# Seven small products spread over a pair of columns, partial sums kept in PSUM and copied by ScalarE

## The chip, the cores and the metric

The kernel runs on one core of a Trainium2 chip. A core has five engines that run side by side and meet at semaphores: TensorE (PE in the profile; PEld is its weight load), VectorE (DVE), ScalarE (ACT), GpSimd (POOL) and SyncE (SP, here only a queue of transfers). Matmuls write to the banks of PSUM; everything else lies in SBUF or in the chip's large memory. The metric is the device time of one execution in microseconds (us). A change is told from no change here when it is over 0.5%.

## The reference

One layer of a hybrid decoder, for 1024 prompt rows and 64 sample rows (T = 1088 columns in the kernel, where rows are laid along the free axis):

```python
h = rmsnorm(x) * (1 + scale) + shift
[u_pool | z_pool | z_ssm | xBC | dt | g] = h @ w_in            # 1024 -> 8224 columns
P = (pool_mix(u_pool) * silu(z_pool)) @ w_pool_out
S = gated_rmsnorm(SSD(conv(xBC)) + D*x, z_ssm) @ w_ssm_out
x = x + gate * ((sigmoid(g_pool) * P + sigmoid(g_ssm) * S) @ w_o)
y = rmsnorm(x)
```

The change lies wholly in the stage that computes `h @ w_in`. All is fp32; a product is made of three products of rounded halves (high by high, high by low, low by high), for which weights and activations are each split in a high and a low part (`whi` and `wlo` for weights).

## The kernel before

**Pairs of columns.** `w_in` is cut into columns of 128. Two columns make a pair, and a pair is computed as a 2 by 2 block product: the two columns, the two halves of the inner dimension (4 tiles of 128 each), and the two halves of T (HF = 544, each again cut into two halves of SB = 272). By Strassen's scheme in Winograd's form seven products do instead of eight. They are named after their weight operand: `b11`, `b21`, `t2`, `t3`, `d12`, `t4`, `b22`. `product` (L430) makes one: for each half `s`, 12 matmuls of 128x128 weights on 272 columns into one bank, and then `use(s, p)` takes the bank's content out. The weight operands are sums of blocks, made by `diff` (L353, on DVE, one on POOL); `split` (L145 on ACT for the high part, L148 on POOL or DVE for the low part) brings them into one of four `whi` and four `wlo` buffers.

**Kinds of pair.** 31 pairs are computed: one inside the opening stage, then `light[1]` and the first of the woven list as plain pairs with seven products (kind None), then 28 that go two by two, a pair of kind "a" and its mate of kind "b". For these the `b21` product is left out of `strassen` (six products), and the `b21` products of both pairs together are made by a second Strassen level: `burst` (L490) computes seven sub-products of six matmuls each, L496, on operands `J` that `joint_operands` prepared. It leaves the part for "a" in `ra` (buffer `c2`) and that for "b" in `rb`. The burst runs as a block of its own ahead of the six products of "a"; its weights are made by `joint_steps` from two loads of their own (`raw`, 256 KB each, one of which holds data that the column's own load brings too).

**Where results go.** In `strassen` (L517) each product's bank is taken out as it ends: `b11` is copied to SBUF by ACT (L532) and, in pairs "a" and "b", added by DVE to `ra` or `rb` (L525); `t2` and `t3` are added by DVE to what stands in SBUF (L520); `d12` and `t4` give outputs (DVE, L525), and `b22` is accumulated on the bank of `d12` ("chained") and gives the last one. Where the destination wants a function (Silu, Sigmoid), ACT applies it in place afterwards (L527). The kernel holds eight PSUM banks in three pools: three `mm` (`PA`), four `ps` (`PB`) and one `pc` (`PC`). Products take them in turn, PA, PB, PA, PB, PA, PB, PC, and in the last ten pairs PB and PA alternately.

**Ticks.** A pair's generator yields after a product. At each yield `between` lets later work of earlier pairs go one step (convolution: L1220 on ACT, three L1223 on DVE, L1228 on ACT) and at `n` = 3, 4, 5 a step of the next pair's weights. A pair "a" yields 10 times, "b" 6 times. Beside the first 20 pairs each yield also moves `splits` (L282, L283 on ACT, L285 on POOL: 40 later weight tiles are split and stored) at a pace of 19/5 ticks a job. Beside the last ten pairs it moves first the preparation of `dt` (14 ticks) and then the sample rows of the state-space branch (`all_samples`, 28 steps); `samples_beside` spreads them by the count `8 * LAST`, with `LAST` = 10.

**Order.** The program is traced in the order of the code, and a scheduler that simulates the engines and goes by priorities lays out each engine's queue; evictions and weight splits have high priority. From tick 14 of the last ten pairs on, PE's order is that of the code (`in_line`). Each engine works off its queue in order.

Of the kernel before, what the change touches and what calls it, by code (L numbers as in the profile page):

```python
# [11 lines left out]
ALU = mybir.AluOpType  # L12
# [34 lines left out]
def tile_pool_ssd_step(  # L47
# [213 lines left out]
    def splits():  # L261
# [68 lines left out]
    def pair_w(c0, c1, pri, apart, meta):  # L330
        def run():
            joint = []
# [21 lines left out]

            def steps():
                add("b11", b11)
# [4 lines left out]
                t4 = raw_()  # L361
                add("t2", t2)
                if meta["kind"] is None:
                    add("b21", b21)
# [9 lines left out]
            def part(x, *names):  # L374
                with tc.high_priority(pri):
                    hi, lo = split(x, highs, n=2 * len(names), eng=V)
                for i, n in enumerate(names):
                    jw[n] = hi[:, 2 * i:2 * i + 2], lo[:, 2 * i:2 * i + 2]

            def joint_steps():  # L380
                wa, wb = joint
                tt = raw_()
                diff(tt[:, 2:4], wb[:, 2:4], wb[:, 0:2])
                diff(tt[:, 0:2], tt[:, 2:4], wa[:, 0:2], ALU.add)
                yield
                part(wa, "b11", "b21")
                diff(wb[:, 0:2], wb[:, 0:2], wa[:, 0:2])
                part(tt, "t2", "t3")
                diff(wa[:, 2:4], tt[:, 0:2], wa[:, 2:4])
                yield  # L390
                part(wb, "d12", "b22")
                part(wa[:, 2:4], "t4")
                yield
# [18 lines left out]
            if apart:  # L412
                add("b11", b11)
                prep_q.append(apart_())
            elif meta["kind"] == "a":
                prep_q.append(joint_steps())
# [2020 lines left out]
```

## Time and profile before

| what | value |
|---|---|
| median of 3 runs | 1271.7 us (1266.74 to 1272.05) |
| the profiled execution, device time | 1262.98 us |
| its span, first to last instruction | 1261.3 us |
| mean granted TensorE clock | 0.993 |
| opening stage (norm, modulation, first pair) | 0 to about 90 us |
| woven pairs (`light[1]` and 19 woven) | about 90 to 556 us |
| last ten pairs, with `dt` and sample rows | about 556 to 803 us |
| chunks of the prompt, output products | 803 us to the end |

The page gives, for each engine, its busy time and share of the span; the groups of instructions give for one line of the code the count, the mean duration, and the idle time of the engine just before them with what ended it. The list of waits sums for each pair of lines how long the first stood idle until the second released it. Matmuls overlap, so that PE's busy time says less than what it waited for.

### The profile page before, as it was taken

Reading aid. Unit: us, or ns where it says so; the run is one execution under the profiler, and the core shown is the slowest. Engines: PE = TensorE matmul, PEld = TensorE weight load, DVE = VectorE, ACT = ScalarE, POOL = GpSimd, SP = SyncE. Lnnn points to the kernel's source line nnn. Section 1 sums busy time; section 2 is a strip of 40 time slices with the busy share of each in tenths; the row PEclk is TensorE's granted clock in tenths of the full one; section 3 lists DMA queues with packets and bytes.
Section 4 is the critical chain, followed back from the end, with each engine's and each line's share of the span. In section 5 each row is a group of like instructions: output and inputs, shape, how many; then the busy total and the mean of one; then the engine's idle time right before and its main releaser. Section 6 shows DMA issues by size and latency. Waiting matters only on the chain.

```text
span 1261.3 us, 25580 instructions
## 1 busy us (share of the span) xinstructions
PE 1206.6 (96%) x9246; PEld 1122.0 (89%) x9246; DVE 1002.8 (80%) x1749; ACT 685.1 (54%) x1561; POOL 724.2 (57%) x649
## 2 busy tenths in 40 slices
PE   9999998999999989988999999899999999999997
PEld 8889998899989989988889889789889898999885
DVE  6998789986998687978676776378687889769976
ACT  6764465566666556555543434455676666411425
POOL 1146659756776855733646656245577668503562
PEclk9999999999999999999999999899999999999999
DMA  9746356466557545544466555779889899676784
GB/s 347 286 146 201 127 160 213 135 207 192 170 167 218 179 154 162 153 131 149 138 228 199 193 195 162 293 246 312 268 239 304 274 273 289 218 268 206 245 200 151
DMA packets 173879, 264.83 MB, mean 210 GB/s; under 512 B 32496, under 2 KB 88568, under 8 KB 173752
## 3 DMA queue, kind: packets, MB, share of 16 engines
q1 hardware_dynamic: 93288, 170.73, 41.8%
q10 hardware_dynamic: 78160, 88.27, 20.7%
q0 software_dynamic: 2304, 4.20, 2.0%
q8 instruction: 73, 1.20, 0.4%
q14 instruction: 54, 0.44, 0.1%
HBM read 178.03 MB, written 85.10 MB: 209 GB/s over the span
## 4 chain that ended last, share of the span: by engine, by line
PE 67%; DVE 9%; issue 4%; DMA 3%; POOL 3%; ACT 2%; SPq 0%; ACTq 0%; DVEq 0%; POOLq 0%
PE mm L221 18%; PE ps L435 13%; PE mm L435 13%; PE ps L1391 3%; PE pc L435 2%; PE pc L1677 2%; PE ps L1394 2%; POOL wlo L148 2%; PE ps L496 2%; PE ps L2190 2%; PE ps L2189 2%; PE ps L2188 2%; PE mm L496 1%; DVE GA L1223 1%; PE ps L1652 1%
## 5 line engine op out<-in xcount | busy, mean ns | idle before, releaser
L221 PE MATMUL mm<-Y,whi 128*128 128x352 f32 (+1 forms) x960 | 197.5, 335 | 6.4 <-DVE R L1873 5.6
L148 POOL TENSOR_TENSOR wlo<-rawA,whi 128x512 fp32r<-128x512 f32 x92 | 147.5, 1605 | 95.8 <-ACT whi L145 70.1
L221 PEld LDWEIGHTS mm<-Y,whi 128*128 128x128 f32 x960 | 160.3, 189 | 13.5 <-DVE R L1873 5.9
L148 POOL TENSOR_TENSOR wlo<-raw,whi 128x512 fp32r<-128x512 f32 x90 | 140.3, 1569 | 21.8 <-ACT whi L145 21.0
L145 ACT ACTIVATE whi<-raw 128x512 fp32r<-128x512 f32 (+1 forms) x146 | 87.0, 605 | 95.5 <-PE ps L435 29.9
L435 PE MATMUL mm<-Y,whi 128*128 128x272 f32 x864 | 128.3, 291 | 8.6 <-DVE c L503 2.4
L435 PE MATMUL ps<-Y,whi 128*128 128x272 f32 x880 | 130.2, 290 | 2.5 <-DVE xd L1422 2.5
L1223 DVE SCALAR_TENSOR_TENSOR GA<-GA,cvT,GA 128x1112 f32<-128x1112 f32 x72 | 128.5, 1789 | 1.3 <-ACT GA L1220 1.3
L435 PEld LDWEIGHTS mm<-Y,whi 128*128 128x128 f32 x864 | 116.0, 189 | 10.7 <-issue 3.7
L435 PEld LDWEIGHTS ps<-Y,whi 128*128 128x128 f32 x880 | 117.6, 188 | 4.2 <-issue 2.9
L221 PE MATMUL mm<-Y,wlo 128*128 128x352 f32 (+1 forms) x480 | 99.1, 328 | 0.0
L145 ACT ACTIVATE whi<-rawA 128x512 fp32r<-128x512 f32 x92 | 57.8, 628 | 69.5 <-PE mm L435 25.2
L1379 ACT ACTIVATE dec<-dec,acT 128x128 f32<-128x128 f32 x256 | 78.8, 389 | 26.8 <-POOL dec L1375 26.7
L285 POOL TENSOR_TENSOR pw<-pw,ph 128x512 fp32r<-128x512 f32 x40 | 69.6, 1740 | 33.5 <-ACT ph L283 33.5
L221 PEld LDWEIGHTS mm<-Y,wlo 128*128 128x128 f32 x480 | 82.2, 189 | 0.0
L435 PE MATMUL mm<-Y,wlo 128*128 128x272 f32 x432 | 73.1, 291 | 5.9 <-POOL wlo L148 5.9
L353 POOL TENSOR_TENSOR raw<-raw,rawA 128x512 f32<-128x512 f32 x30 | 44.4, 1481 | 57.7 <-DVE wlo L148 31.9
L435 PE MATMUL ps<-Y,wlo 128*128 128x272 f32 x440 | 73.8, 289 | 2.6 <-POOL wlo L148 2.6
L1609 POOL TENSOR_TENSOR Y<-xb,Y 128x512 fp32r<-128x512 f32 x32 | 41.1, 1285 | 52.5 <-ACT Y L1607 52.4
L435 PEld LDWEIGHTS mm<-Y,wlo 128*128 128x128 f32 x432 | 61.2, 189 | 7.3 <-POOL wlo L148 7.3
L435 PEld LDWEIGHTS ps<-Y,wlo 128*128 128x128 f32 x440 | 61.9, 188 | 3.3 <-POOL wlo L148 3.3
L1670 DVE TENSOR_TENSOR dec<-dec,ps 128x1024 f32<-128x1024 f32 x32 | 38.9, 1216 | 27.6 <-ACT ps L1659 10.4
(658 smaller groups left out, 3288.3 us busy)
## 6 DMA issues: line engine op xcount, KB each, us to landing
rawA<-in_w_in SPq DMA_DIRECT2D x62, 512.0 KB
dec<-acs_d SPq DMA_DIRECT2D x32, 512.0 KB
xbc<-GA ACTq DMA_DIRECT2D x24, 512.0 KB
Y<-wo SPq DMA_DIRECT2D x10, 1024.0 KB
raw<-in_w_in SPq DMA_DIRECT2D x32, 256.0 KB
pw<-in_w_ssm_out ACTq DMA_DIRECT2D x32, 256.0 KB
ws<-ph ACTq DMA_DIRECT2D x32, 256.0 KB
ws<-pw ACTq DMA_DIRECT2D x32, 256.0 KB
```

Of the source, the lines that this page charges most:

```text
L145: ins = act(hi[:, :n], raw, AF.Copy)
L148: (eng or nc.gpsimd).tensor_tensor(lo[:, :n], raw, hi[:, :n].bitcast(F32), ALU.subtract)
L221: mm(ps[:, :n], w[k // 4][h][:, k % 4, :], r[k][:, o:o + n], start=(j == 0), stop=(j == len(terms) - 1))
L285: nc.gpsimd.tensor_tensor(raw.bitcast(F32R), raw, hi.bitcast(F32), ALU.subtract)
L353: eng.tensor_tensor(dst, x, y, op)
L435: mm(p, w[j // 8][:, k], A(k, s)[j // 4 == 1], start=(j == 0 and not on), stop=(j == 11), skip_group_check=bool(on))
L496: mm(p, w[n][j // 4][:, k], A(k)[j // 2 == 1], start=(j == 0 and on is None), stop=(j == 5), skip_group_check=on is not None)
L1223: V.scalar_tensor_tensor(d[:, :n], rp[:, k:k + n], cvT[:, 24 * k + mc:24 * k + mc + 1], d[:, :n], ALU.mult, ALU.add)
L1379: act(dec[:, h], dec[:, h], AF.Exp, bias=acT[:, c, 8 * g + h:8 * g + h + 1], scale=-1.0)
L1391: mm(o[hh], xd[:S, 2 * q + hh, :], dec[:S, 2 * q + hh], start=True, stop=state is None)
L1609: nc.gpsimd.tensor_tensor(yl[g][:, :, o:o + S], v, yhc.bitcast(F32), ALU.subtract)
L1670: V.tensor_tensor(dec, dec, pbc[:, P:2 * P].unsqueeze(1).to_broadcast([P, 8, P]), ALU.mult)
```

## The change

The burst is no block any more. Its seven sub-products are made in five steps (one or two each) that `strassen_j` calls between the six products of pair "a". The products `b11`, `t2`, `t3`, `t4` of a pair "a" or "b" accumulate on the same two banks (`on`, from `PA`): before the next product is added to a bank, ACT copies its present content to SBUF (`save`), so that the sum that DVE made in SBUF is made by the matmul in PSUM. The sign of `t4` is turned for that, and its result is taken out by ACT with the function applied (`evict`). The sub-products are chained in one bank `q` in the same way. In a pair "a" the addition of `b11` and `ra` is done by POOL from SBUF. In the last ten pairs ("not chained") `d12` comes after `t3` and `b22` has banks of its own. Pairs of kind None get `b21` in a bank of its own.

The weight operands of the burst come from the column's own load and one `raw` load. A pair "a" yields six times, as "b" does; the pace of `splits` is 14/5 and the sample rows are spread by `6 * LAST`. The bank of two helpers changes: `u_unit` takes `PC` and yields between its three matmul groups, and `update` of the sample rows takes `PB, PB, PB, PC`.

```diff
-                at.setdefault(n * 19 // 5 + step, []).append((f, n))
+                at.setdefault(n * 14 // 5 + step, []).append((f, n))
...
-                if meta["kind"] == "a":
-                    for c in (c0, meta["mate"]):
-                        r = raw_()
-                        load(r, tiles_of(c)[:, 4:8])
-                        joint.append(r)
...
+                if kind == "a":
+                    wb = raw_()
+                    load(wb, tiles_of(meta["mate"])[:, 4:8])
...
+            def steps_j():
+                late = not meta["chained"]
+                if kind == "a":
+                    part(b21, "b11", "b21")
+                add("b11", b11)
+                t3 = raw_()
+                diff(t3, b22, b12)
+                if kind == "a":
+                    tt = raw_()
+                    diff(tt[:, 2:4], wb[:, 2:4], wb[:, 0:2])
+                    diff(tt[:, 0:2], tt[:, 2:4], b21[:, 0:2], ALU.add)
+                yield
+                if kind == "a":
+                    part(tt, "t2", "t3")
+                diff(b12, b12, b11)
+                if not late:
+                    add("d12", b12)
+                add("t3", t3)
+                diff(t3, t3, b11, ALU.add)
+                add("t2", t3)
+                yield
...
+                diff(b21, b21, t3, eng=nc.gpsimd)
+                add("t4", b21)
...
-        b1 = sub("b11", "a11", keep)
-        sub("t2", "s2", add(rb[:, 0], ra[:, 0]))
-        yield
-        sub("b21", "a12", keep, on=b1)
-        sub("t3", "s3", add(ra[:, 1], rb[:, 0]))
-        yield
-        b4 = sub("d12", "s1", add(rb[:, 1], ra[:, 1]))
-        sub("t4", "a22", add(ra[:, 1], ra[:, 1], ALU.subtract))
-        yield
-        sub("b22", "s4", add(rb[:, 0], rb[:, 0]), on=b4)
+        q = sub("b11", "a11", keep(ra[:, 0]))
+        sub("b21", "a12", add(ra[:, 0], ra[:, 0]))
+        yield
+        sub("t2", "s2", keep(rb[:, 0]), q)
+        yield
+        sub("t3", "s3", keep(ra[:, 1]), q)
+        yield
+        g = sub("d12", "s1", fifth)
+        sub("t4", "a22", keep(ra[:, 1]), q)
+        yield
+        sub("b22", "s4", add(rb[:, 0], rb[:, 0]), g if chained else None)
+        yield
...
+    def evict(d, o, buf):
+        def use(s, p):
+            def put(dst, a=0, b=SB, v=lambda t: t, func=None):
+                act(dst, v(p[:, a:b]), AF.Copy if func is None else func)
+            d(o + SB * s, SB, put, buf)
+        return use
...
+    def save(x):
+        return lambda s, p: act(x[:, s], p, AF.Copy)
...
+    def strassen_j(w, d0, d1, r, subs, chained):
+        if subs is not None:
+            next(subs)
+        s1, u2, u3 = tmp("s1"), tmp("u2"), tmp("u3")
+        on = [PA()[:, :SB] for _ in range(2)]
+        fresh = lambda: [PB()[:, :SB] for _ in range(2)]
+
+        def first_(s, p):
+            if subs is None:
+                out(d0, 0, r, r)(s, p)
+            else:
+                save(s1)(s, p)
+
+        def mark(s, p):
+            save(u3)(s, p)
+            if chained:
+                out(d1, HF, u3, u3)(s, on5[s])
+
+        def fifth(s, p):
+            if not chained:
+                out(d1, HF, u3, u3)(s, p)
+                sums(u2, u2)(s, p)
+        product(w["b11"], a_part(0, 0), first_, on, True)
+        yield
+        if subs is not None:
+            next(subs)
+        on5 = fresh() if chained else None
+        if chained:
+            product(w["d12"], s_part(S1), fifth, on5, True)
+        else:
+            product(w["t2"], s_part(S2), save(u2), on)
+        yield
+        if subs is not None:
+            next(subs)
+        if chained:
+            product(w["t2"], s_part(S2), save(u2), on)
+        else:
+            product(w["t3"], s_part(S3), mark, on)
+        yield
+        if chained:
+            product(w["t3"], s_part(S3), mark, on)
+        else:
+            product(w["d12"], s_part(S1), fifth, fresh(), True)
+        yield
+        if subs is not None:
+            next(subs)
+            with tc.high_priority(PRI):
+                for s in range(2):
+                    out(d0, 0, s1, r, eng=nc.gpsimd)(s, r[:, s])
+        product(w["t4"], a_part(1, 1), evict(d0, HF, s1), on)
+        yield
+        if subs is not None:
+            next(subs)
+        product(w["b22"], s4_part, out(d1, 0, u2, u2), on5 if chained else fresh(), not chained)
...
-            ps = PB()
+            ps = PC()
...
-            pus = [p()[:, :256] for p in (PB, PA, PB, PA)]
+            pus = [p()[:, :256] for p in (PB, PB, PB, PC)]
...
-        if due[0] == 8 * LAST - 4:
+        if due[0] == 6 * LAST - 4:
...
-        while made_[0] < (due[0] - FIRST) * 4 * SSTEPS / (8 * LAST - FIRST - SPARE):
+        while made_[0] < (due[0] - FIRST) * 4 * SSTEPS / (6 * LAST - FIRST - SPARE):
```

More of the change, by code (lines that the diff above doesn't have):

```diff
@@ L427, in bank_, with product @@
         return banks_[0][turn[0] % len(banks_[0])]()[:, :SB]
-    def product(w, A, use, on=None):
-        ps = []
+    def product(w, A, use, on=None, first=False):
+        first = first or on is None
         for s in range(2):
@@ L567, in run @@
         def run(w):
-            w, jw, prep, steps = w
+            w, jw, prep = w
             prep_q.remove(prep)
@@ L573, in run @@
             kind = meta["kind"]
[L574 to L577 removed]
+            ds = [next(it) for it in its]
+            if kind is None:
+                main = strassen(w, *ds)
+            elif kind == "a":
                 ra, rb = tmp("c2"), tmp("rb")
                 r_next.append(rb)
[L580 to L593 removed]
+                main = strassen_j(w, *ds, ra, burst(jw, ra, rb, meta["chained"]), meta["chained"])
+            else:
+                main = strassen_j(w, *ds, r_next.pop(), None, meta["chained"])
+            for n, _ in enumerate(main):
                 if meta.get("mark") and n == 2:
                     rest_[0] = True
[L596 removed]
+                between(n + (kind is not None and n > 1))
                 yield
```

142 lines of the change are left out of this document (56 added, 86 removed).

## The prediction

> **What bounds the kernel now.** I read the page's engine line first, then the busy times by stage, then TensorE's waits.
>
> ```profile
> PE 1206.6 (96%) x9246; PEld 1122.0 (89%) x9246; DVE 1002.8 (80%) x1749; ACT 685.1 (54%) x1561; POOL 724.2 (57%) x649
> ```
>
> TensorE bounds the kernel. By stage (start and end, length, then for PE, PEld, DVE, ACT and POOL the busy us with instructions, the granted clock, the DMA share and GB/s):
>
> ```profile
> 250.00:300.00 50.00, 50.00 (x400) 49.97 (x400) 36.73 (x65) 33.92 (x81) 35.60 (x24) 1.00 0.64 203
> 90.00:556.00 466.00, 443.43 (x3423) 434.83 (x3423) 391.15 (x616) 268.11 (x620) 323.09 (x211) 0.99 0.55 173
> 556.00:803.00 247.00, 234.41 (x1887) 217.88 (x1887) 175.15 (x383) 117.38 (x238) 136.89 (x135) 1.00 0.55 185
> ```
>
> The first stretch is one without a stall: 400 matmuls in 50 us, 125 ns each. So a half product (12 matmuls) takes 1.5 us. The change keeps the number of matmuls, so that only idle time can go: 466 - 443.4 = 22.6 us in the woven pairs and 247 - 234.4 = 12.6 us in the last ten. What ended it, first for the woven pairs, then for the last ten (us in total, times, longest):
>
> ```profile
> PE mm L435 <- POOL wlo L148: 5.9, 5, 2.7
> PE ps L435 <- POOL wlo L148: 4.0, 5, 1.6
> PE pc L435 <- DVE GA L525: 2.5, 1, 2.5
> PE mm L435 <- DVE c L503: 2.4, 1, 2.4
> PE mm L435 <- DVE s L525: 2.4, 1, 2.4
> ...
> PE mm L435 <- ACT c L506: 1.1, 1, 1.1
> PE mm L496 <- DVE rb L503: 1.0, 2, 0.8
> PE pc L496 <- ACT c L506: 0.5, 1, 0.5
> PE mm L435 <- DVE GA L525: 0.3, 1, 0.3
> ```
>
> ```profile
> PE mm L496 <- ACT c L506: 2.7, 1, 2.7
> ...
> PE ps L435 <- DVE xd L1422: 2.5, 2, 1.7
> ...
> PE mm L435 <- DVE u L520: 0.7, 1, 0.7
> PE mm L435 <- DVE rb L503: 0.5, 1, 0.5
> PE mm L435 <- DVE rb L525: 0.5, 1, 0.5
> ```
>
> In the woven pairs late evictions cost 8.6 (DVE) + 1.6 (ACT) = 10.2 us and late low halves of weights 9.9 us. In the last ten, evictions cost 2.7 + 0.7 + 0.5 + 0.5 = 4.4 us, and sample work for which DVE was late 2.5 us. Behind most of it stands DVE, busy 391 of 466 us (84%) in the woven pairs.
>
> **What is taken from DVE and given to ACT and POOL.** Counting evictions per half: a chained pair "a" has 17 on DVE before and 7 after, a chained "b" 12 and 6, in the last ten 19 and 10, 14 and 8; each of the two plain pairs gets 4 more. That is 9x10 + 9x6 + 5x9 + 5x6 - 8 = 211 fewer. ACT gets 8 more per "a" and 4 per "b", 168, less some 28 (functions now applied in the eviction, a plain pair's copies).
>
> ```profile
> L520 DVE TENSOR_TENSOR u<-u,ps 128x272 f32<-128x272 f32 x37 | 15.9, 429 | 13.9 <-PE ps L435 13.9
> L532 ACT ACTIVATE s<-ps 128x272 f32<-128x272 f32 x28 | 10.7, 382 | 4.4 <-POOL pw L285 2.6 <-PE ps L435 1.7
> L1610 POOL TENSOR_TENSOR sz<-sz x32: 724/734/760, 833.2 to 1099.9; 128x256 f32<-128x256 f32 x32
> ```
>
> DVE loses 211 x 0.43 = 91 us, ACT gains 140 x 0.38 = 53 us. POOL gains 28 additions of 272 columns, by the row for 256 an estimated 0.78 us each, 22 us. In the woven pairs DVE falls from 84 to some 71%, ACT rises from 58 to some 65%. I take it that
>
> - the woven evictions' 10.2 us go whole, since banks outside the chain come back sooner;
> - of the 9.9 us for low halves 5 go (bounds 0 and 9.9): POOL's split follows a DVE difference and an ACT rounding, and DVE's part comes sooner;
> - the 4.4 us in the last ten go, and half of the 2.5 us for sample work, 1.2.
>
> Together **20.8 us gained**, at most 27.0.
>
> POOL's time depends on what DVE does beside it (POOL, then DVE, twice):
>
> ```profile
> 508.21 4.66 POOL L148 TENSOR_TENSOR wlo<-raw,whi 128x512 fp32r<-128x512 f32 x2
> 509.35 2.38 DVE L1223 SCALAR_TENSOR_TENSOR GA<-GA,cvT,GA 128x1112 f32<-128x1112 f32 x1
> ```
>
> ```profile
> 415.34 2.55 POOL L148 TENSOR_TENSOR wlo<-raw,whi 128x512 fp32r<-128x512 f32 x2
> 416.20 0.44 DVE L525 TENSOR_TENSOR GA<-c,ps 128x272 f32<-128x272 f32 x1 [1.76 <-ACT s L532]
> ```
>
> Two splits took 4.66 us beside a convolution step and 2.55 us beside an eviction. [...]
>
> **The chain's price.** A product that adds to bank `on` waits for ACT's copy of what stands there. For each half the other half's 1.5 us lie between, and a matmul ends some 0.16 us after the next one has started (two in a row take 0.41 us in the row of 506.33 below: 0.125 and 0.285), so that some 1.33 us are left. No more lies between `t2` and `t3` in each of the 9 woven "a", between `t2` and `t3` and between `t3` and `t4` in each woven "b", and twice in each "b" of the last ten: 27 + 10 tight steps. (In "a" a sub-product, in the last ten a sample step lies in most of the others.) How prompt is ACT now? Both ends, the half product's last matmuls and then its copy (start, us; PE and ACT):
>
> ```profile
> 506.33 0.41 PE L435 MATMUL ps<-Y,wlo 128*128 128x272 f32 x2
> ...
> 507.59 1.27 ACT L282 ACTIVATE pw<-pw,vT 128x128 f32<-128x128 f32 x4
> ...
> 508.76 0.38 ACT L532 ACTIVATE s<-mm 128x272 f32<-128x272 f32 x1
> 509.56 0.38 ACT L532 ACTIVATE s<-ps 128x272 f32<-128x272 f32 x1
> ```
>
> ```profile
> 785.63 0.67 PE L435 MATMUL mm<-Y,wlo 128*128 128x272 f32 x4
> ...
> 786.33 0.40 ACT L532 ACTIVATE s<-mm 128x272 f32<-128x272 f32 x1 [0.62 <-PE mm L435]
> ```
>
> In the woven pairs (first) the product ended at 506.74 and its copy at 509.94, 3.20 us later, behind four scalings of `splits` and the copy of the other half; in the last ten (second) it took 786.73 - 786.30 = 0.43 us. So a tight step costs between 0 and 3.20 - 1.33 = 1.9 us. Before, nobody waited for such a copy, as seven banks went round. I take one woven step in eight at 1.9, because ACT is idle 42% of that stage and the scheduler can put a sub-product in the gap: 27 x 0.24 = **6.4 us lost** (bounds 0 and, half of them late, 26). In the last ten, 10 x 0.1 = **1 us**. What waits behind a late copy on ACT are weight splits (L145), and PE waits for those later; that is part of the 1.9.
>
> **The bank of the sample rows.** `state` writes `pc`, ACT copies it (L1500), and `update` follows at once in PE's fixed order; now its fourth matmul takes `pc` too:
>
> ```profile
> 618.14 1.06 PE L1479 MATMUL pc<-h,cz 128*32 128x512 f32 x8
> 619.35 0.60 ACT L1500 ACTIVATE hT<-pc 128x512 f32<-128x512 f32 x1 [0.92 <-PE pc L1479]
> ```
>
> From the end at 619.20 to the copy's end at 619.95 PE stands: 0.75 us, 8 times, **6.0 us lost** (bounds 3, if the wait covers others, and 12, if ACT is late).
>
> **The rest, at nothing.** 14 loads of 256 KB fewer: DMA is at 0.55 in these stages and no wait on `raw` is among PE's. `splits` has 122 ticks instead of 158 and a pace of 2.8 instead of 3.8 ticks a job, the same rate in time. Later work (convolution) loses four ticks per "a" and is flushed at the pair's end; the DVE time set free covers it, without which 56 steps of L1223 would come late. The 28 sample steps go into 39 ticks of equal length instead of 59 shorter ones; PE has the same work. `u_unit` on `PC` with yields between: 12 matmul groups apart, nothing. POOL's 22 us lie beside its 143 idle us of the woven pairs.
>
> **The sum.** -20.8 + 6.4 + 1 + 6.0 = -7.4 us. Against the profiled execution (1262.98 us, span 1261.3) that gives 1256; the median of the runs shown stands 8.7 us above it, and I carry the difference over: 1271.7 - 7.4, rounded, **1264 us**, 0.6% less. The measurement tells 0.5%, 6.4 us.
>
> **The rivals.**
>
> - *ScalarE becomes the clock of the chain* (slower). Place: the woven pairs' 27 steps. Without them the sum is -13.8, so the change loses as soon as 27% of the steps wait 1.9 us, and loses 0.5% from 39%. At half of them it is -13.8 + 26 = +12, 1284 us. For it: ACT goes to 65%, and the copies above came 2.9 and 3.2 us late. Against it: the copies in the last ten are prompt.
> - *DVE was the cause of nearly all stalls* (faster). The whole 27 us go and the chain costs 2: -27 + 2 + 1 + 6 = -18, 1254 us. For it: 84% busy DVE in the stage; against it: low halves are split on POOL.
> - *An exchange of waits*: the low halves stay late and one chain step in five waits: -15.8 + 10 + 1 + 6 = +1, 1273 us. [...]
>
> [...]
>
> **How the numbers follow.** Forecast 0.40 (1258 to 1271: 0.25 faster, 0.15 same); ScalarE's chain 0.24 (0.22 slower, 0.02 same); DVE the cause 0.20 (faster); exchange 0.16 (0.14 same, 0.02 slower). Faster 0.45, same 0.31, slower 0.24. The forecast's own range is 1258 to 1271; to hold both outer cases I take 1248 (27 us gone and only the bank's lower bound of 3 lost) to 1284 (half the chain late).
>
> **What would show it.** Right: DVE near 71% and ACT near 65% between 90 us and the end of the woven pairs; PE's waits on L503, L520 and L525 gone; new waits of PE on the `save` copies of ACT, some 6 us in all; eight waits of 0.75 us at `update` on `pc`. Wrong: over 15 us of PE waits on ACT copies, POOL's waits unchanged or longer, or PE idle on weights because the splits stand behind copies in ACT's queue.

## The result and the profile after

The changed kernel takes **1308.1 us** (median of 4 runs, 1304.78 to 1313.09) beside 1271.9 us (1266.74 to 1273.87) for the kernel before on the same chip: ratio 1.0295, 95% interval 1.0248 to 1.0341. It is 36 us slower, where 7 us faster was forecast. The profiled execution is the slowest of the four (1313.09 us, span 1311.4), so the profile shows 50 us of difference in span and the medians 36: the profiled execution of the kernel before (1262.98 us, granted clock 0.993) is faster than every other execution of it on record (1263.9 to 1280.7 us).

The engine line of the page after, and the slices of the granted clock:

```profile
PE 1229.6 (94%) x9246; PEld 1139.5 (87%) x9246; DVE 941.7 (72%) x1523; ACT 727.6 (55%) x1716; POOL 731.9 (56%) x677
...
PEclk9999999999999999999999889989999999999999
```

DVE lost 61 us of busy time and 226 instructions, ACT gained 42.5 us, POOL 8. The relief is there. But TensorE, with the same 9246 matmuls, is busy 23 us longer, and three slices show 8 in the clock's line.

The busy times by stage give the place. Start and end, length, then PE, PEld, DVE, ACT, POOL busy, granted clock, DMA share, GB/s; cut at the same matmul in both kernels (the first line of each is the woven pairs, the second the last ten). Before:

```profile
90.30:543.60 453.30, 431.45 (x3332) 423.29 (x3331) 380.86 (x595) 261.62 (x606) 314.00 (x200) 0.99 0.55 173
543.60:802.80 259.20, 245.89 (x1974) 228.92 (x1973) 185.00 (x404) 123.41 (x251) 145.69 (x145) 1.00 0.55 183
```

After:

```profile
90.30:563.80 473.50, 437.04 (x3333) 425.59 (x3332) 340.78 (x441) 292.87 (x720) 312.91 (x219) 0.99 0.51 160
563.80:852.30 288.50, 262.52 (x1974) 243.30 (x1973) 161.23 (x331) 136.40 (x293) 153.22 (x154) 0.95 0.49 161
```

The woven pairs are 20.2 us longer, the last ten 29.3 us; what follows is the same length (458.5 and 459.1 us). In each stage the time splits in two. TensorE's **idle** time (length less busy) goes from 21.9 to 36.5 us in the woven pairs and from 13.3 to 26.0 in the last ten, 27.3 us in all. The rest, 22.2 us, is busy time for the same matmuls, and most of it is the **clock**: over the span the mean granted clock fell from 0.993 to 0.980, for which I estimate from the two spans, counting time as lost in proportion to the clock, 1311.4 x 0.020 - 1261.3 x 0.007 = 17.4 us. The other 5 us I can't attribute. But these two executions are the ends of their kernels: over the executions of the five groups of runs below, the kernel before has a median clock of 0.987 (16.5 us lost to it), and the four of the changed kernel have 0.980 to 0.984 (22.8 us at the median). So of the 36 us between the medians the clock is, by this estimate, some 6.

What TensorE waited for after, in the woven pairs (us in total, times, longest):

```profile
PE mm L446 <- ACT whi L145: 10.8, 5, 4.2
PE mm L446 <- POOL wlo L148: 8.0, 6, 2.8
PE ps L507 <- ACT whi L145: 5.8, 4, 2.6
PE mm L446 <- ACT u L556: 3.8, 3, 2.0
PE ps L446 <- ACT whi L145: 1.6, 1, 1.6
PE ps L507 <- DVE wlo L148: 1.2, 2, 1.0
PE ps L446 <- DVE GA L549: 1.2, 3, 0.7
PE ps L446 <- DVE u L549: 0.7, 1, 0.7
...
PE mm L446 <- DVE GA L549: 0.5, 1, 0.5
```

The late evictions of before are mostly gone: DVE's (L549) are 1.2 + 0.7 + 0.5 = 2.4 us here, and no further row of theirs is over 0.4 us. The chain's copies (L556) cost 3.8 us. New are 10.8 + 5.8 + 1.6 = 18.2 us for **high halves of weights** (`whi`); the list before, cut at the same matmul, has one such row:

```profile
PE mm L435 <- ACT whi L145: 1.1, 2, 0.6
```

And in the last ten, after:

```profile
PE pc L1550 <- ACT hT L1562: 5.3, 7, 1.4
PE pc L507 <- DVE h L1557: 3.6, 1, 3.6
PE ps L446 <- DVE h L1557: 3.1, 1, 3.1
PE ps L1491 <- DVE xd L1484: 2.5, 3, 1.3
PE ps L446 <- DVE dec L1526: 2.2, 1, 2.2
PE ps L446 <- ACT whi L145: 1.9, 1, 1.9
PE ps L1550 <- DVE u L544: 1.8, 2, 1.6
...
PE mm L507 <- ACT c L517: 0.7, 1, 0.7
PE ps L507 <- DVE u L544: 0.6, 1, 0.6
```

Here the price of the bank stands first, 5.3 us. Then come products and sub-products that wait until DVE has taken `update`'s result out of a bank (`h`, L1557, 6.7 us), then sample work and weights.

Why are the high halves late? DVE's own waits for the differences (L351) in the woven pairs, after:

```profile
DVE raw L351 <- DMA rawA<-in_w_in: 28.1, 11, 4.0
DVE raw L351 <- POOL wlo L148: 18.9, 10, 5.8
```

The second row has no counterpart in DVE's list of before. The new `steps_j` writes `t2` into the tile in which `t3` stands, so the difference has to wait until POOL has split `t3`; and it writes `t4` into the block `b21` of the column's own buffer, so that buffer stays in use until `t4` is split, and the next column's load lands late (the first row: ten of its eleven loads were issued when POOL had just ended a split of a column's block). Before, `t2` and `t4` had tiles of their own. The longest of TensorE's waits for a high half, in order of time:

```profile
412.68 1.31 POOL L148 TENSOR_TENSOR wlo<-raw,whi 128x512 fp32r<-128x512 f32 x1
...
413.63 2.82 DVE L1285 SCALAR_TENSOR_TENSOR GA<-GA,cvT,GA 128x1112 f32<-128x1112 f32 x2
...
416.38 1.75 DVE L351 TENSOR_TENSOR raw<-raw,rawA 128x512 f32<-128x512 f32 x1
...
418.22 0.63 ACT L145 ACTIVATE whi<-raw 128x512 fp32r<-128x512 f32 x1 [1.19 <-DVE GA L1267]
...
418.90 0.52 PE L446 MATMUL mm<-Y,whi 128*128 128x272 f32 x2 [4.23 <-ACT whi L145]
```

POOL's split frees the tile at 413.99; two convolution steps stand before the difference in DVE's queue; the difference ends at 418.13, ACT rounds it, and TensorE, idle for 4.23 us by then, starts at 418.90. So the tile had been free for 2.4 us when the difference began: this stall ended with DVE's queue. (The profile puts ACT's wait down to L1267, a clearing of three columns on DVE that ended at 418.14 with the difference.) One step further back, TensorE's eleven waits for high halves in this stage (18.6 us with one of 0.4) part. In one of 2.9 us the difference itself had waited for POOL's split:

```profile
364.65 1.74 DVE L351 TENSOR_TENSOR raw<-raw,rawA 128x512 f32<-128x512 f32 x1 [1.59 <-POOL wlo L148]
```

In five (9.8 us) the difference came straight behind other work of DVE, four times a convolution step; in five (6.0 us) the rounding came straight behind other work of ACT. So the trace shows that the operands in place hold DVE up, but not that most stalls end with that wait; what they cost is for the runs to show.

The window after the longest stall (columns as above) shows the second price:

```profile
419.50:422.90 3.40, 3.40 (x17) 3.40 (x16) 0.00 (x0) 2.31 (x6) 3.40 (x3) 0.50 0.65 214
```

For 3.40 us after the stall the granted clock is 0.50, and 17 matmuls take the time of 27: at 125 ns each (400 in 50 us in the prediction's first stretch), the stall of 4.2 us costs an estimated 1.3 us more by this count, and at most 1.7, half of the window.

### The profile page after: what moved, and what is told of

Same layout as the page of the kernel before. It is cut to its first block, busy times and chain, and to the rows that moved or that the text cites. A ratio compares the mean times of both kernels' runs of the same rounds, so it can differ in the third digit from the quotient of the medians.

```text
span 1311.4 us, 25310 instructions
## 1 busy us (share of the span) xinstructions
PE 1229.6 (94%) x9246; PEld 1139.5 (87%) x9246; DVE 941.7 (72%) x1523; ACT 727.6 (55%) x1716; POOL 731.9 (56%) x677
## 5 line engine op out<-in xcount | busy, mean ns | idle before, releaser
L148 POOL TENSOR_TENSOR wlo<-rawA,whi 128x512 fp32r<-128x512 f32 x120 | 170.3, 1423 | 149.2 <-ACT whi L145 125.5
L446 PE MATMUL mm<-Y,whi 128*128 128x272 f32 x1392 | 211.5, 295 | 13.5 <-ACT whi L145 12.1
L446 PEld LDWEIGHTS mm<-Y,whi 128*128 128x128 f32 x1392 | 191.3, 193 | 18.2 <-ACT whi L145 13.8
L221 PEld LDWEIGHTS mm<-Y,whi 128*128 128x128 f32 x960 | 160.4, 189 | 14.2 <-DVE R L1935 5.8
L446 PE MATMUL mm<-Y,wlo 128*128 128x272 f32 x696 | 117.6, 294 | 9.7 <-POOL wlo L148 9.7
L145 ACT ACTIVATE whi<-rawA 128x512 fp32r<-128x512 f32 x134 | 83.4, 627 | 71.0 <-PE ps L446 17.4
L148 POOL TENSOR_TENSOR wlo<-raw,whi 128x512 fp32r<-128x512 f32 x62 | 97.7, 1576 | 34.6 <-ACT whi L145 23.7
L446 PE MATMUL ps<-Y,whi 128*128 128x272 f32 x496 | 75.5, 295 | 5.3 <-DVE dec L1526 2.2
L285 POOL TENSOR_TENSOR pw<-pw,ph 128x512 fp32r<-128x512 f32 x40 | 62.2, 1556 | 30.4 <-ACT ph L283 19.7
L446 PE MATMUL mm<-G,whi 128*128 128x272 f32 x480 | 71.6, 292 | 3.7 <-ACT u L556 3.5
L446 PEld LDWEIGHTS ps<-Y,whi 128*128 128x128 f32 x496 | 67.7, 193 | 7.2 <-DVE dec L1526 2.4
L148 DVE TENSOR_TENSOR wlo<-raw,whi 128x512 fp32r<-128x512 f32 (+1 forms) x42 | 42.7, 1016 | 42.1 <-ACT whi L145 20.8
L446 PE MATMUL ps<-R,whi 128*128 128x272 f32 x348 | 64.2, 297 | 6.6 <-ACT whi L145 3.5
L446 PEld LDWEIGHTS mm<-G,whi 128*128 128x128 f32 x480 | 65.2, 192 | 4.4 <-ACT u L556 4.3
```

What stands on the lines that cost most here:

```text
L145: ins = act(hi[:, :n], raw, AF.Copy)
L148: (eng or nc.gpsimd).tensor_tensor(lo[:, :n], raw, hi[:, :n].bitcast(F32), ALU.subtract)
L221: mm(ps[:, :n], w[k // 4][h][:, k % 4, :], r[k][:, o:o + n], start=(j == 0), stop=(j == len(terms) - 1))
L285: nc.gpsimd.tensor_tensor(raw.bitcast(F32R), raw, hi.bitcast(F32), ALU.subtract)
L446: mm(p, w[j // 8][:, k], A(k, s)[j // 4 == 1], start=(j == 0 and first), stop=(j == 11), skip_group_check=not first)
```

## The experiments

My theory: weights prepared too late, because of the operands in place, and windows at a granted clock of 0.50 after long stalls, like the one of 3.40 us above. The rivals: ScalarE's copies (the chain), the bank of the sample rows, the new order of the sub-products, the denser ticks. A last pair of runs tests the length of DVE's convolution steps.

All kernels here compute the whole of the reference. In the table, "woven" and "last" are the stages' lengths in the profile, cut as above; "idle" is the sum of TensorE's waits of over 0.2 us in the two stages, "half" the time in both at a granted clock of 0.50, both added up from the trace. These four figures are of one execution each, and the one of the kernel before is its best.

| kernel | median us | ratio to before, interval | woven, last | idle | half |
|---|---|---|---|---|---|
| before | 1271.9 | | 453.3, 259.2 | 34.9 | 6.8 |
| after | 1308.1 | 1.0295 (1.0248 to 1.0341) | 473.5, 288.5 | 61.9 | 41.0 |
| e1 after, `t2` elsewhere | 1301.6 | 1.0239 (1.0187 to 1.0292) | 469.5, 277.4 | 51.9 | 37.5 |
| e2 e1, and `t4` elsewhere | 1293.0 | 1.0169 (1.0128 to 1.0210) | 466.6, 274.2 | 48.3 | 30.7 |
| e3 after without the chain | 1309.5 | 1.0296 (1.0245 to 1.0346) | 480.0, 276.8 | 56.4 | 37.5 |
| e4 after, `update` without `PC` | 1320.3 | 1.0383 (1.0339 to 1.0427) | 476.8, 291.8 | 66.0 | 58.0 |
| e5 e2 without the chain | 1293.1 | 1.0184 (1.0143 to 1.0225) | 465.5, 273.8 | 48.8 | 23.9 |
| e7 e2, chain in woven pairs only | 1291.8 | 1.0174 (1.0136 to 1.0213) | 469.1, 267.9 | 44.1 | 34.1 |
| e8 before, operands in place, `t2` a step later | 1295.7 | 1.0205 (1.0168 to 1.0242) | 475.2, 268.0 | 53.8 | 51.2 |
| e9 before, `pc` in `update` | 1275.6 | 1.0040 (1.0012 to 1.0068) | 455.3, 269.2 | 37.7 | 23.9 |
| e10 e7, sample steps thinner | 1296.8 | 1.0203 (1.0169 to 1.0237) | 469.0, 276.5 | 50.8 | 41.0 |
| e11 e2, more ticks for later work | 1297.4 | 1.0212 (1.0176 to 1.0247) | 471.1, 276.5 | 49.1 | 47.8 |
| e12 before, sample steps denser | 1277.8 | 1.0068 (1.0046 to 1.0090) | 454.2, 268.3 | 37.2 | 17.1 |
| e13 before, chain alone | 1288.7 | 1.0141 (1.0113 to 1.0170) | 474.7, 261.0 | 45.4 | 37.5 |
| e14 before, spread alone | 1290.6 | 1.0153 (1.0117 to 1.0189) | 472.5, 265.6 | 43.6 | 37.5 |
| e15 before, pace of `splits` 18/5 | 1276.4 | 1.0034 (1.0010 to 1.0058) | 461.0, 264.5 | 35.7 | 27.3 |
| e16 before, `u_unit` on `PC` | 1274.3 | 1.0017 (0.9989 to 1.0045) | 455.6, 265.3 | 36.9 | 17.1 |
| e17 e13, copies by DVE | 1288.9 | 1.0144 (1.0108 to 1.0179) | 472.7, 263.6 | 48.6 | 30.7 |
| e18 e2, convolution steps halved | 1301.5 | 1.0238 (1.0190 to 1.0287) | 475.7, 277.3 | 52.5 | 44.4 |
| e19 before, convolution steps halved | 1290.0 | 1.0172 (1.0120 to 1.0224) | 473.6, 271.0 | 47.0 | 47.8 |

The kernel before in the five groups of runs (e1 to e4, e5 to e9, e10 to e13, e14 to e17, e18 and e19): 1270.9, 1269.1, 1269.7, 1272.2 and 1268.5 us.

**e1 and e2: the operands out of each other's way.** `t2` goes into the block `b11`, whose content nobody needs by then (though the block lies in the column's buffer, too), and in e2 `t4` goes into `t3`'s tile rather than the column's buffer.

```diff
-                diff(t3, t3, b11, ALU.add)
-                add("t2", t3)
+                diff(b11, t3, b11, ALU.add)
+                add("t2", b11)
...
-                diff(b21, b21, t3, eng=nc.gpsimd)
-                add("t4", b21)
+                diff(t3, b21, b11, eng=nc.gpsimd)
+                add("t4", t3)
```

> The changed kernel, but t2 is written into the block of b11 and not into the tile of t3, so that it need not wait until POOL has split t3. Theory W (weight operands in place make the weights late): VectorE's 18.9 us of waits on POOL's splits go, most of TensorE's 21.8 us of waits on ScalarE's weight roundings in the woven pairs go with them, the time falls by 10 to 20 us from the 1308 us of the changed kernel. Theory C (the chain through ScalarE copies is the cause): within 5 us of 1308.

> As the run before, and t4 is written into the tile of t3, so that the first column's buffer is free when t4 has been computed, not when it has been split. Theory W: the waits of VectorE on column loads (29.2 us in the changed kernel) fall by half or more and the time falls by another 3 to 10 us. If the column's buffer was not what held the weights: no change against the run before.

e1 gives back 7 us, both together 15 us of the 36 (medians; the interval of e1's ratio overlaps that of the changed kernel, e2's doesn't). TensorE's waits for high halves in the woven pairs fall from 18.6 to 4.9 us in e1 and 3.5 in e2; in e1 those for POOL's low halves rise from 8.4 to 13.4. TensorE's waits in e2, woven pairs:

```profile
PE mm L446 <- POOL wlo L148: 7.4, 5, 3.3
PE mm L446 <- ACT u L556: 6.0, 6, 2.5
...
PE ps L507 <- ACT whi L145: 2.6, 3, 1.5
```

The long waits for high halves are gone, and so is DVE's wait for POOL at L351. Its wait for the column loads is not: 28.1 us in the changed kernel, 36.8 in e1, 21.1 in e2, where half or less was expected. The column's buffer is still held, now by `t2`, which stands in its block `b11`. What stays, 21 us, is spread over many short rows, the copies' 6.0 us among them.

**e3, e4, e5, e7: without the chain, and without `pc`.** e3 takes the chain out of the changed kernel (banks in turn, sums by DVE as before, `update` on its old banks); e4 keeps the chain and puts `update` wholly on `PB`; e5 is e3 with the operands of e2; e7 is e2 with the chain in the woven pairs alone and `update` on its old banks.

```diff
-            product(w["t2"], s_part(S2), save(u2), on)
+            product(w["t2"], s_part(S2), sums(s1, u2))
...
-            pus = [p()[:, :256] for p in (PB, PB, PB, PC)]
+            pus = [p()[:, :256] for p in (PB, PA, PB, PA)]
```

> The changed kernel without the chain: every product and sub-product gets a bank in turn as before the change, VectorE adds the partial sums, the update of the sample rows has its old banks; the sub-products stay spread and the weights stay as changed. Theory C: the time falls to 1275 us or less. Theory W: the woven pairs (473 us in the changed kernel's profile) stay over 465 us, and only the last ten gain, by the 5 to 20 us that banks cost there.

> The changed kernel with the four banks of update taken from PB, none from PC. If the bank of the sample rows costs what the profile shows (5.3 us of waits, and half-clock windows after them): 5 to 15 us less than the changed kernel, all of it in the last ten pairs. If the pressure only moves to PB: no gain or a loss.

> The changed kernel with both mended weight operands (t2 in the block of b11, t4 in the tile of t3), and without the chain and the bank choices, so that only the spread sub-products, the shared load and the new ticks are left of the change. If weights and banks are all that costs: 1271 us, as before the change, or less. If spreading the sub-products with six ticks a pair costs by itself: 1280 us or more, with waits in both stages.

> Mended weight operands; the chain in the woven pairs, banks in turn and VectorE's sums in the last ten, with the old banks for update. If the chain's banks are what slows the last ten: the last ten fall from 274 us to some 265, and the time from 1293 us to 1285 or less. If not: 1290 or more.

Taking the chain out gains nothing: 1309.5 beside 1308.1, and with the operands mended 1293.1 beside 1293.0. In e5 no wait for a copy stands in the list, but the banks come back late another way (woven pairs):

```profile
PE pc L505 <- DVE GA L550: 5.0, 2, 2.6
...
PE pc L446 <- DVE GA L550: 2.8, 1, 2.8
```

e4 lost 12 us more: without `pc` nobody waits for `hT`, but products wait for `PB`, which DVE empties (last ten):

```profile
PE ps L446 <- DVE h L1557: 8.0, 5, 3.1
PE ps L507 <- DVE h L1557: 5.6, 2, 3.5
```

So with two `PA` banks held by the chain, `PC` was a less bad place for `update` than `PB` alone. e7 puts `update` back and takes the chain out of the last ten: these get 6 us shorter than in e2 in the profile, the median 1 us less, which these runs don't tell from nothing.

**e8, e9, e12: single parts on the kernel before.** e8 gives the kernel before the in-place operands (`t3` is then split ahead of `t2`, and `t2`'s difference moves from the first step to the second, as in the changed kernel); e9 the banks of `update`; e12 packs the 28 sample steps into fewer ticks.

```diff
-                t3, t2 = raw_(), raw_()
+                t3 = raw_()
...
+                diff(t3, t3, b11, ALU.add)
+                add("t2", t3)
...
-                diff(t4, t2, b21, eng=nc.gpsimd)
+                diff(b21, t3, b21, eng=nc.gpsimd)
```

```diff
-            pus = [p()[:, :256] for p in (PB, PA, PB, PA)]
+            pus = [p()[:, :256] for p in (PB, PB, PB, PC)]
```

```diff
-    SPARE = 7
+    SPARE = 15
```

> The kernel before, in which alone t2 is written into the tile of t3 after t3 has been split, and t4 into the column's block. Theory W: TensorE's waits on weight roundings and low halves grow and the kernel loses 8 to 20 us against 1271. If in-place operands cost only together with the spread sub-products: within 4 us.

> The kernel before, in which alone update takes PB, PB, PB, PC. By the term of the prediction: 8 waits of 0.75 us on the copy out of pc, 4 to 10 us more, all in the last ten pairs. If the wait is covered: within 3 us.

> The kernel before, in which alone the 28 sample steps are spread over 51 ticks instead of 59, which gives them the density in time that they have after the change. If density is a cause: 4 to 10 us over 1270, in the last ten pairs, with half-clock windows. If not: within 3 us.

e8 alone costs 27 us (ratio 1.0205). Its waits, and its busy times, in the woven pairs:

```profile
PE mm L434 <- ACT whi L145: 14.2, 3, 5.9
PE pc L434 <- DVE c L502: 9.4, 2, 4.9
PE ps L434 <- ACT whi L145: 4.3, 2, 4.0
```

```profile
89.70:564.90 475.20, 439.63 (x3332) 433.48 (x3331) 376.66 (x596) 263.90 (x607) 299.02 (x200) 0.96 0.52 166
```

14.2 + 4.3 = 18.5 us for high halves, as in the changed kernel, 9.4 us for the burst's sums (`c`), and a clock of 0.96 in place of 0.99: the stage is 21.9 us longer with no chain, no spread, and as many instructions on each engine as before. In the four longest waits for a high half (18.2 us) POOL had ended its last split 1.0 to 4.7 us before DVE came to the difference, behind other work of its queue. So e8 prices the place and the later step together, and no run has the later step alone. e9 costs 6.4 us between the medians (interval of the ratio 1.0012 to 1.0068, 1.5 to 8.6 us), with the waits that the prediction named:

```profile
PE pc L1488 <- ACT hT L1500: 3.7, 8, 0.5
```

e12 costs 8.2 us, where the prediction put the denser steps at nothing.

**e13, e17, e14: chain alone, and spread alone.** e13 puts the chained banks, with ScalarE's copies, the turned sign of `t4` and other banks for the burst, into the chained pairs of the kernel before; e17 is e13 with DVE copying `t2` and `t3` (ACT still takes `t4` out); e14 has the new order (sub-products between the products, six ticks, the addition on POOL, the shared load) with DVE's sums, with the operands of e2 and with `t2` split ahead of `t3`.

```diff
+        product(w["t2"], s_part(S2), save(u2), on)
...
+        product(w["t3"], s_part(S3), save(u3), on)
```

```diff
-            return lambda s, p: act(x[:, s], p, AF.Copy)
+            return lambda s, p: V.tensor_copy(x[:, s], p)
```

> The kernel before, in which alone the woven pairs a and b keep t2, t3 and t4 on the banks of b11, ScalarE copying between; burst, weights and ticks as before. By the prediction's terms for the woven pairs, -10 us for late evictions, up to -5 for weights and +6 for the chain: 1259 to 1270 us. Theory C (late ScalarE copies): 1280 us or more, with over 10 us of waits on these copies.

> The kernel before with the chain in the woven pairs, VectorE copying t2 and t3 out of the banks instead of ScalarE. If ScalarE's load makes the weights late: 1275 us or less, from 1289. If the chain's order or the weights' queue does, whoever copies: 1285 us or more.

> Only the spread of the sub-products is left of the change: products in the old order with VectorE's sums and banks in turn, weights without operands in place and split in the order of use, six ticks a pair, POOL's addition. If spreading is harmless: 1266 to 1276 us. If it costs by itself (denser sample steps, bunched evictions): 1280 us or more.

Each costs some 18 us: 19 (e13), 17 (e17), 18 (e14). e13's waits in the woven pairs, and its busy times there:

```profile
PE mm L439 <- POOL wlo L148: 9.0, 5, 5.4
PE mm L439 <- DVE GA L1248: 6.8, 3, 4.1
PE ps L439 <- ACT whi L145: 5.5, 3, 2.8
```

```profile
90.70:565.40 474.70, 440.66 (x3332) 431.84 (x3332) 352.25 (x474) 285.50 (x689) 308.08 (x200) 0.97 0.52 165
```

DVE is busy 28.6 us less than before in this stage, and the stage is 21.4 us longer. None of the leading rows is a copy: late are weights (9.0 + 5.5 = 14.5 us) and, behind the rows of L1248, evictions. The longest of those (4.07 us, in order of time):

```profile
192.81 4.35 DVE L1266 SCALAR_TENSOR_TENSOR GA<-GA,cvT,GA 128x1112 f32<-128x1112 f32 x2
...
193.65 4.64 POOL L148 TENSOR_TENSOR wlo<-raw,whi 128x512 fp32r<-128x512 f32 x2
...
197.08 0.42 DVE L578 TENSOR_TENSOR GA<-c,mm 128x272 f32<-128x272 f32 x1
```

The bank `mm` is free when the eviction ends at 197.50, and that has stood behind two convolution steps, which take 4.35 us beside POOL's splits. (L1248, a clearing of three columns, is only what ended on DVE last.) e17 hands the copies to DVE and comes out the same (intervals 1.0113 to 1.0170 and 1.0108 to 1.0179), so the chain's price doesn't depend on ScalarE's making them. In e14 the rows are the same kind:

```profile
PE mm L442 <- POOL wlo L148: 5.8, 2, 4.0
PE mm L501 <- DVE wlo L148: 4.3, 3, 1.9
```

**e10, e11: repairs that did not help.** e10 starts the sample steps earlier (`dt` in 9 ticks, two steps at once, so that the 28 steps have 45 ticks); e11 gives the later work a further step beside each sub-product.

```diff
-    FIRST = 14
+    FIRST = 9
```

```diff
+            between("j")
```

> The run with the chain in the woven pairs only, in which the preparation of dt takes 9 ticks instead of 14 (two steps in each of the first five) and the 28 sample steps spread over 45 ticks instead of 39. If the density of the sample steps slows the last ten: the waits on the additions to h (5.9 us) fall under 3 us and the time by 5 to 10 us from 1292 us. If not: within 3 us.

> Mended weight operands with the chain, and one step of later work (convolution) after each of the five groups of sub-products, as the burst's ticks gave before. If the bunching of later work at the pair's end is what is left in the woven pairs: they fall from 467 to some 458 us, the time from 1293 to some 1285 us. If not: within 3 us.

Both medians lie 4 to 5 us above their base (1296.8 beside 1291.8, 1297.4 beside 1293.0; the intervals of the ratios overlap), so neither is a repair. The thinning of the sample steps does not undo in the new order what e12 cost in the old one, so e12's 8 us stand for the kernel before alone.

**e15 and e16: a control, and `u_unit`.** e15 changes the pace of `splits` in the kernel before from 19/5 to 18/5 ticks, with the same work; e16 gives it `u_unit` on `PC` with the yields.

```diff
-                at.setdefault(n * 19 // 5 + step, []).append((f, n))
+                at.setdefault(n * 18 // 5 + step, []).append((f, n))
```

> The kernel before with the pace of the 40 later weight tiles at 18/5 ticks a job instead of 19/5: the same work, a little earlier. A measure of how much the time moves with any change of the order. If the kernel is robust: within 4 us of 1270. If it is finely balanced: 5 to 15 us more, by late weights and half-clock windows.

> The kernel before with u_unit's three matmul groups on PC and a step between them, as the change has it. By the prediction nothing: within 4 us of 1270. If PE waits for ScalarE's evictions of pc: 3 to 8 us more.

e16 is no change that can be told. The control costs 4 us (1.0010 to 1.0058) with TensorE idle no longer in its profile (35.7 us beside 34.9). The half clock there, 27.3 us beside 6.8, is set against the best execution of the kernel before; the median clocks of the two in this group are 0.986 and 0.987, about 1 us apart, so the place of the 4 us is open. So some 4 us is what laying the same work out in another way can cost this kernel, and a part that costs little more, as e9, is known by its waits rather than by its median.

**e18 and e19: shorter steps on DVE.** In two of the stalls shown, two convolution steps stood ahead of the short instruction that TensorE's work waited for. Here each is cut in two, in e2's kernel and in the kernel before.

```diff
-            V.scalar_tensor_tensor(d[:, :n], rp[:, k:k + n], cvT[:, 24 * k + mc:24 * k + mc + 1], d[:, :n],
-                                   ALU.mult, ALU.add)
+            for a, b in ((0, 556), (556, n)):
+                V.scalar_tensor_tensor(d[:, a:b], rp[:, k + a:k + b], cvT[:, 24 * k + mc:24 * k + mc + 1], d[:, a:b],
+                                       ALU.mult, ALU.add)
```

> The changed kernel with t2 in b11's block and t4 in t3's tile, and with each DVE convolution step (128x1112, 1.36 us alone and 2.2 us beside POOL) cut into two of 128x556. In two stalls of over 4 us (one of the changed kernel, one of the kernel before with the chain alone) two such steps stood ahead of the short instruction that TensorE's work waited for, a difference in one and an eviction in the other. If this blocking in DVE's queue is what is left of the loss, the median falls from 1293 to 1285 us or less and TensorE's idle time in the pair stages from 48 to 40 us or less. If it is only the place where lateness from elsewhere shows (too little lead of the weights, held banks), it stays within 4 us of 1293 and the idle time within 4 us of 48.

> The kernel before with the same halved convolution steps, as the control. Here no stall of over 3 us stands behind such a step, so both theories expect it within 5 us of the kernel before, 0.4%, which is about what another layout of the same work costs. A gain of over 5 us would mean that the blocking costs the kernel before as well, and then a gain in the other run says nothing of the change.

Both got slower, by 8 us (e18 beside e2) and by 21 us (e19), which neither theory expected. The reason the runs don't decide is in the group's row, first of the kernel before, then of e19:

```profile
L1223 DVE SCALAR_TENSOR_TENSOR GA<-GA,cvT,GA 128x1112 f32<-128x1112 f32 x72 | 128.5, 1789 | 1.3 <-ACT GA L1220 1.3
```

```profile
L1224 DVE SCALAR_TENSOR_TENSOR GA<-GA,cvT,GA 128x556 f32<-128x556 f32 x144 | 168.0, 1203 | 1.3 <-ACT GA L1220 1.3
```

Half a step takes 1.20 us, not 0.89, so that DVE got 39.5 us more work. Blocking and load are both in the result. What e19 does show: a change without chain, spread, bank or operands, which gives DVE more work, loses as much as the chain or the spread alone.

No version here beat the kernel before.

## Why the prediction was wrong

**The step that failed** is "The rest, at nothing", with the hope of 5 us before it. The prediction counted what the new preparation of weights saves (loads) and nothing of the new waits inside it. It followed the waits of the chain and of the bank, but not those of `diff(t3, t3, b11, ALU.add)` and `diff(b21, b21, t3, eng=nc.gpsimd)`, which stood in the diff. Shown: undoing the two gives back 15 us of the 36 (e1, e2), and TensorE's waits for high halves go from 18.6 to 3.5 us; doing them in the kernel before, with the later step that they came with, costs 27 us (e8). By which of the queues each stall ended is another matter: the wait for POOL's split was the last in one of eleven. The denser sample steps stood in the same paragraph at nothing, and cost the kernel before 8 us (e12); `u_unit` on `PC` was rightly put at nothing (e16).

**The clock** was no term at all. In the two profiles the added half-clock time of the pair stages, 41.0 - 6.8 = 34.2 us at a granted clock of 0.50, is an estimated 17.1 us, nearly the 17.4 of above; by the median clocks it is some 6 us of the 36. By the same reckoning the median clock of e8 (0.976) costs 15 us, of e14 (0.979) 11, of e13 (0.981) 8.

Term by term, by the waits of the two profiles:

- Woven evictions, 10.2 us gained: mostly right, DVE's rows fell from 8.6 to 2.4 us, with 0.7 more in two smaller ones.
- Low halves, 5 us gained: wrong. They cost 9.9 us before and 8.0 + 1.2 = 9.2 us after, with DVE at 72% as at 84%. The term looked to DVE's part and not to POOL's queue: in four of POOL's waits (6.7 of 8.0 us) the split stood straight behind a job of `splits` (L285), in the kernel before in three (4.7 us).
- Evictions and sample work in the last ten, 4.4 + 1.2 us gained: wrong. Evictions (`c` L517, `u` L544) cost 1.8 + 0.7 + 0.6 = 3.1 us still, `xd` still 2.5 us, and `h` and `dec` 8.9 us; the waits for `h`, 6.7 us, come where the chain holds two `PA` banks and `update` takes `PB`, whose later users the term for `pc` left out (e9, with these banks and no chain, has no such row over 0.2 us).
- The chain, 6.4 us lost: 3.8 us by its own waits; the size of these was right. In the last ten they are 0.6 us, in rows below those shown, and 1 us had been put down. But the chain as a whole was not: by the prediction's terms e13, the chain alone in the woven pairs, was to take 1259 to 1270 us, and it took 1288.7.
- The bank, 6.0 us lost: 5.3 us, seven of eight waits. Right, by mechanism and size; e9 shows the same wait eight times, at 3.7 us in all.

The gap before the fourth matmul came as forecast, 0.48 us here where 0.75 had been put down (start, us; PE and ACT, after): three matmuls of `update`, ACT's copy of `pc`, and the fourth matmul.

```profile
654.37 0.39 PE L1550 MATMUL ps<-dec 32*128 32x256 f32 x3
654.58 0.60 ACT L1562 ACTIVATE hT<-pc 128x512 f32<-128x512 f32 x1 [0.63 <-PE pc L1541]
655.23 0.38 PE L1550 MATMUL pc<-dec 32*128 32x256 f32 x1 [0.48 <-ACT hT L1562]
```

**The signs named beforehand.** DVE at 72% of the woven pairs (71 forecast) and ACT at 62% (65) look right, but in part by luck: they are shares of a longer stage, in which DVE lost 40 us where 60 had been forecast. The count of evictions was sound: added up from the traces, DVE's went from 474 to 248 (211 fewer forecast) and lost 93 us (91 forecast). But the 56 low halves that DVE makes (L148) took 57.0 us instead of 37.8, which takes back 19. And the relief of DVE was not worth what it was taken for. "PE idle on weights" was named as a sign that the prediction is wrong, and came, but for another reason than the one given (splits behind copies in ACT's queue): in the stall shown, ACT stood idle for 1.19 us until DVE had made the difference, and in the five where the rounding came straight behind other work of ACT, that was in no case one of the chain's copies.

**The rivals.** ScalarE's chain was the one on the slower side, and the result lies beyond it (1284). It is not what happened: its copies are 3.8 us, and neither taking the chain out (e3, e5) nor giving the copies to DVE (e17) moves the time. Exchange and DVE as the cause of all are out by size.

**What stays open.** After the mended operands 21 us are left. The chain alone and the spread alone each cost nearly as much (19 and 18), and taking the chain out of both again gains nothing. The single parts on the kernel before (27, 19, 18, 6 and 8 us for e8, e13, e14, e9, e12) add up to 78 us, over twice what all together cost; e14 has denser sample steps too, but even without e12's 8 us they don't add. e19 loses 21 us with none of these parts. So those 21 us can't be given to one of them; the kernel before stands where each of several disturbances costs 17 to 27 us, and by the lists above weights and evictions then come late at several places. One part was in every kernel with the changed weights (e2, e5, e14, and e8) and was never run alone: `t2`'s difference made in the second step and not in the first. Why there is so little lead, I can only argue: there are four `whi` and four `wlo` buffers, and DVE takes short urgent work and long convolution steps in one order. More buffers, and convolution steps on another engine, were not tried.

## What to carry to other kernels

When an operand is built in the place of another, list what must have read the old one, what stands on the queues in between, and which load then waits for the buffer: here that cost more than the tile it saved. Price a long stall of TensorE with the slow stretch after it: here a window at a granted clock of 0.50, of 3.4 us or more, followed all 40 stalls of 3 us or more. Freeing an engine that isn't the bound (DVE, busy 40 us less in the woven pairs) gained here no more than the waits that it ended last (its evictions, from 8.6 to 2.4 us); put each part of a large change on the kernel before by itself, and a change of layout that does nothing beside them, before adding up. And take the clock from many executions: two profiles gave 17 us here, the medians 6.

## What was not expected of the hardware

The half clock came after short stalls. In the pair stages of the 20 traces here, all 40 stretches of 3 us or more in which TensorE ran no matmul were followed (from their start to 3.5 us after their end) by a window at a granted clock of 0.50; of those of 2 to 3 us 65 of 94 were, of 1 to 2 us 53 of 231, of those from 0.2 to 1 us 32 of 425. A window is 3.4 us, or twice that, once three times. So the stalls that it followed here were often shorter than one window: of the 190 so followed, 150 were under 3 us.

And a DVE instruction cut in two cost a third more in e18 (two halves of 1.24 us on average beside 1.87 for a whole step in e2) and e19 (two of 1.20 beside 1.79): in e19 of the 144 halves the shortest took 0.78 us, the median 0.79, the longest 1.92, with a mean of 1.20. The prediction's rows had shown that POOL is slowed beside such steps (two splits took 4.66 us beside one, 2.55 beside an eviction); here it is seen that DVE is too. In the kernel before, 16 of the 72 whole steps had no POOL work beside them and took 1.37 us on average, the other 56 took 1.91. In e19, 56 halves alone took 0.79 us and the other 88 took 1.47. So two halves alone cost 0.2 us more than one whole, and a half beside POOL paid 0.68 us extra, more than a whole step's 0.54.
